# A two-layer diffusion backbone in fp32: the modulation's background steps on another timetable, half of the norm roots on VectorE

## The chip, the cores and the metric

The kernel runs on one core of one Trainium2 chip, as one launch. The metric is the device time of that launch in microseconds. Engines are called as the profile does: PE is TensorE, DVE is VectorE, ACT is ScalarE, POOL is GpSimd, SP is SyncE.

## The reference

Two layers of a backbone for flow matching work on 256 context tokens followed by 512 latent tokens, width 1024, feed-forward width 2816. Each layer has a SwiGLU feed-forward half step, a token mixer, and a second feed-forward half step. Layer 0 mixes with windowed attention beside a chunked spatial gating (gMLP), layer 1 with a bidirectional recurrence. Each of these three parts begins with an RMS norm and is modulated by three vectors (shift, scale, gate) that come from the conditioning vector through a large weight matrix `ada_w` of 1024 x 9216 per layer:

```python
def rmsnorm(x, g):
    xf = x.astype(jnp.float32)
    y = xf * lax.rsqrt(jnp.mean(xf * xf, axis=-1, keepdims=True) + EPS)
    return (y * g.astype(jnp.float32)).astype(x.dtype)

def modulate(h, shift, scale):
    return h * (1.0 + scale) + shift

def ffn_half_step(x, g, shift, scale, gate, wg, wu, wd):
    h = modulate(rmsnorm(x, g), shift, scale)
    return x + 0.5 * gate * swiglu(h, wg, wu, wd)
```

Context tokens use a learned conditioning vector `c_ctx`, so there are two versions of each modulation vector.

## The kernel before, in words

**Products.** All matrices are fp32. `mm3` (L124 ff) makes one product out of three matmuls of high and low halves (`hhi`, `hlo` of the activations, two halves of each weight tile `w`). Most are 128 x 384: the 768 tokens are worked on in two halves, `TA` (tokens 0 to 383) and `TB` (384 to 767). Weights are streamed: SP loads a `raw` chunk (L188), ACT and DVE split it into halves (L198 and L201, or seven combinations in `Seven`, L228 to L245), in a pool of twelve slots. `stream["limit"]` says how many of them may be in use.

**Order.** The program is written out by a Python planner. `mm` adds an estimated time to a clock `clk.t`; after each `mm3`, `clk.tick()` runs the jobs that are due on a heap. Steps of weight preparation, parts of a norm, and the background steps described next are such jobs, so what is written when follows this estimated time. The framework then arranges each engine's instructions once more (one whose inputs are there early can come to stand ahead of others that were written before it); the rows quoted below show that final order, in which each engine runs them.

**Modulation in the background.** `ada_jobs` (L465 ff) computes the modulation vectors (l, m), m from 0 to 8, one after the other in the order of `ada_halves`: layer 0 as 2, 4, 3, 5, 7, 6, 8 (0 and 1 are made at the start), then layer 1. Each needs eight tiles `aw` of 512 KB, loaded by SP into two buffers (`ada_load`), and 32 steps on DVE that multiply a tile by one conditioning value and add it into `acc` (L494, L496, 128 x 512), then transposes and sums (L505, L506) into `red`. `finish` closes a vector: one small matmul of `red` with `quarters` into `ps`, and four additions (L479). `ada_event` (L521 ff) runs one step and puts itself back on the heap: each 1600 ns of planned time until (0,2) is done, then each `bg["every"]`. Whoever needs a vector calls `mod(l, m)` (L527 ff), which runs all the steps that are still missing at that place:

```python
    def mod(l, m):
        while mods_done.get((l, m), 0) < 4:
            ada_step()
        return mods[l][:, m]
```

**Feed-forward.** `ffn(l, j, ...)` (L652 ff) works through groups of the 22 column blocks: products `pgu` for gate and up, `g` on DVE (L682), `ghi`/`glo` (L135, L136), then `down` with products `pd`, whose result is multiplied by the gate vector `gate`. That vector is made at the first `down` by `gates(l, m, .5)` (L643), which calls `mod`; ffn (0,0) needs (0,2), ffn (0,1) needs (0,8). Sums of scaled activations called `form` (L708 to L731) are made on DVE for the products that use seven combinations. In the last group `bg["on"]` is set False, and the next norm is fed.

**Norm.** `Norm` (L545 ff) sums squares, then `stats` (L574 ff) makes the inverse root with `rsqrt` (L142 ff): three operations on DVE and three rounds of Newton's method, each round four operations on POOL (L150, L155, L156, L157), or three on DVE (L150, L152, L153) where the caller asks for it. `spread` takes the root `rstd` to all partitions through TensorE, `apply` and `halve` make the halves. The last `halve` of the second half sets `bg["on"] = not bg["hold"]`.

**Attention and gMLP.** `even_mixer` (L896 ff) has 24 attention units; each ends with a multiplication of the result by the weights of the softmax (L1132, tile `q`), called a gather here. Between them stand the gMLP's row blocks with a root `rs_z` of their own on DVE. In the main program (L1486) the background is switched on with `hold=True`, which stops it when norm (0,1) is through; it stays off through most of the attention.

## Time and profile before

| | |
|---|---|
| median of 3 runs | 2626.02 us (2624.25 to 2627.23) |
| profiled execution | 2622.59 us |
| its span | 2620.8 us |
| mean granted TensorE clock | 0.985 |
| PE busy | 2529.3 us (97%), 14370 matmuls |
| DVE busy | 1869.7 us (71%) |
| ACT busy | 1249.0 us (48%) |
| POOL busy | 238.8 us (9%) |
| DMA | 328.45 MB, 125 GB/s |

The page divides one execution by engine, by line and by wait. A row of a timeline gives the start of an instruction (or of a run of equal ones, with the number behind x), its duration, the engine, the line, output and inputs, and in brackets the idle time ahead of it with the engine and tile that ended it. A granted clock of 1.00 is 2.4 GHz, .50 is 1.2 GHz.

### The profile page before, as it was taken

Reading aid. Unit: us, or ns where it says so; the run is one execution under the profiler, and the core shown is the slowest. Engines: PE = TensorE matmul, PEld = TensorE weight load, DVE = VectorE, ACT = ScalarE, POOL = GpSimd, SP = SyncE. Lnnn points to the kernel's source line nnn. Section 1 sums busy time; section 2 is a strip of 40 time slices with the busy share of each in tenths; the row PEclk is TensorE's granted clock in tenths of the full one; section 3 lists DMA queues with packets and bytes.
Section 4 is the critical chain, followed back from the end, with each engine's and each line's share of the span. In section 5 each row is a group of like instructions: output and inputs, shape, how many; then the busy total and the mean of one; then the engine's idle time right before and its main releaser. Section 6 shows DMA issues by size and latency. Waiting matters only on the chain.

```text
span 2620.8 us, 37768 instructions
## 1 busy us (share of the span) xinstructions
PE 2529.3 (97%) x14370; PEld 2352.3 (90%) x14370; DVE 1869.7 (71%) x3590; ACT 1249.0 (48%) x2433; POOL 238.8 (9%) x389
## 2 busy tenths in 40 slices
PE   8799999999999997999999999999999999999998
PEld 5799999998899996999999889999999988888887
DVE  7778878787668687867768888765467898544444
ACT  3344544545556353444454444444545996433322
POOL 0021012200000002012120020121300000000000
PEclk9999999999999998999999999999999999999999
DMA  9266467653011417556675165673642123322221
GB/s 324 89 144 164 138 157 177 169 172 113 1 33 42 151 51 166 159 142 145 157 165 187 39 176 169 171 191 92 134 145 81 49 75 102 107 97 97 94 89 57
DMA packets 248430, 328.45 MB, mean 125 GB/s; under 512 B 19985, under 2 KB 172729, under 8 KB 247737
## 3 DMA queue, kind: packets, MB, share of 16 engines
q1 hardware_dynamic: 213264, 278.69, 32.8%
q0 software_dynamic: 34560, 47.20, 12.3%
q8 instruction: 112, 1.84, 0.3%
q14 instruction: 70, 0.57, 0.1%
q10 hardware_dynamic: 424, 0.15, 0.0%
HBM read 262.04 MB, written 63.96 MB: 124 GB/s over the span
## 4 chain that ended last, share of the span: by engine, by line
PE 73%; issue 12%; DVE 7%; ACT 4%; POOL 3%; DMA 1%; ACTq 0%; POOLq 0%; DVEq 0%
PE pgu L121 22%; PE pd L121 20%; PE seeded L121 13%; PE ps L121 10%; PE po L121 4%; POOL kept L696 2%; PE pv L121 1%; PE sl L121 1%; PE sc L121 1%; DVE acc L496 1%; PE pt L1111 1%; ACT w L198 1%; DVE w L201 1%; PE pre L121 1%; DVE hlo L607 0%
## 5 line engine op out<-in xcount | busy, mean ns | idle before, releaser
L121 PE MATMUL pd<-ghi,w 128*128 128x256 f32 (+2 forms) x2528 | 649.6, 344 | 2.3 <-ACT ghi L135 2.2
L121 PE MATMUL pgu<-hhi,w 128*128 128x384 f32 (+2 forms) x2144 | 594.5, 349 | 0.9 <-ACT hhi L601 0.6
L121 PEld LDWEIGHTS pd<-ghi,w 128*128 128x128 f32 x2528 | 443.3, 190 | 53.7 <-ACT ghi L135 4.2
L121 PE MATMUL pd<-glo,w 128*128 128x256 f32 (+2 forms) x1264 | 433.6, 344 | 0.8 <-DVE glo L136 0.8
L121 PEld LDWEIGHTS pgu<-hhi,w 128*128 128x128 f32 x2144 | 392.0, 189 | 27.8 <-ACT hhi L601 1.3
L121 PE MATMUL pgu<-hlo,w 128*128 128x384 f32 (+2 forms) x1072 | 374.1, 349 | 1.3 <-DVE hlo L607 1.2
L201 DVE TENSOR_TENSOR w<-raw,w 128x512 fp32r<-128x512 f32 x404 | 271.5, 686 | 92.6 <-ACT w L198 90.1
L198 ACT ACTIVATE w<-raw 128x512 fp32r<-128x512 f32 x404 | 245.7, 626 | 180.4 <-PE pd L121 79.1
L696 POOL DMA_DIRECT2D kept<-add x240 | 208.2, 900 | 1158.7 <-ACT add L695 1150.4
L496 DVE SCALAR_TENSOR_TENSOR acc<-aw,cs,acc 128x512 f32<-128x512 f32 x392 | 280.4, 744 | 33.0 <-DMA aw<-in_ada_w_dram 32.1
L228 DVE TENSOR_TENSOR w<-raw,w 128x512 fp32r<-128x512 f32 x348 | 232.1, 685 | 91.9 <-ACT w L245 88.8
L695 ACT ACTIVATE add<-pd,gate 128x256 f32<-128x256 f32 x240 | 138.7, 580 | 278.0 <-PE pd L121 234.5
L121 PEld LDWEIGHTS pd<-glo,w 128*128 128x128 f32 x1264 | 239.9, 190 | 27.4 <-DVE glo L136 3.2
L121 PE MATMUL seeded<-form,w 128*128 128x384 f32 x1392 | 261.6, 335 | 2.6 <-ACT seeded L790 2.5
L121 PE MATMUL seeded<-hhi,w 128*128 128x384 f32 x928 | 247.8, 335 | 1.4 <-ACT hhi L135 1.0
L121 PEld LDWEIGHTS seeded<-form,w 128*128 128x128 f32 x1392 | 243.1, 188 | 3.5 <-ACT seeded L790 2.8
L245 ACT ACTIVATE w<-raw 128x512 fp32r<-128x512 f32 x348 | 207.1, 627 | 58.4 <-DVE raw L244 17.6
L121 PEld LDWEIGHTS pgu<-hlo,w 128*128 128x128 f32 x1072 | 202.4, 189 | 15.3 <-DVE hlo L607 2.1
L121 PE MATMUL ps<-hhi,w 128*128 128x384 f32 (+1 forms) x704 | 197.6, 355 | 7.6 <-ACT t L1327 6.2
L121 PEld LDWEIGHTS seeded<-hhi,w 128*128 128x128 f32 x928 | 168.6, 188 | 3.4 <-ACT hhi L135 2.5
L121 PE MATMUL seeded<-hlo,w 128*128 128x384 f32 x464 | 155.3, 335 | 0.4 <-DVE hlo L136 0.4
L121 PEld LDWEIGHTS ps<-hhi,w 128*128 128x128 f32 x704 | 132.1, 193 | 15.4 <-ACT t L1327 7.2
(302 smaller groups left out, 3645.0 us busy)
## 6 DMA issues: line engine op xcount, KB each, us to landing
aw<-in_ada_w_dram SPq DMA_DIRECT2D x128, 512.0 KB, 5.2
raw<-in_ffn_w_gate_dram SPq DMA_DIRECT2D x44, 1024.0 KB, 5.6
raw<-in_ffn_w_up_dram SPq DMA_DIRECT2D x44, 1024.0 KB, 5.3
raw<-in_ffn_w_down_dram SPq DMA_DIRECT2D x40, 1024.0 KB, 5.2
kept<-add POOLq DMA_DIRECT2D x120, 256.0 KB, 5.4
kept<-add POOLq DMA_DIRECT2D x120, 128.0 KB, 5.6
x<-kept SPq DMA_DIRECT2D x48, 192.0 KB, 4.2
fw<-in_ada_w_dram SPq DMA_DIRECT2D x16, 512.0 KB, 8.8
```

The source lines that it names most:

```text
L121: pe.matmul(o, w, x, start=start, stop=stop, skip_group_check=again)
L198: act.activation(tiles[i][:, 0:512], self.raw[:, i * 512:i * 512 + 512], AF.Copy)
L201: dve.tensor_tensor(t[:, 512:1024], self.raw[:, i * 512 - 512:i * 512], t[:, 0:512].bitcast(F32), op=ALU.subtract)
L228: dve.tensor_tensor(l, src[key], h.bitcast(F32), op=ALU.subtract)
L245: act.activation(halves_of(key)[0], src[key], AF.Copy)
L496: dve.scalar_tensor_tensor(acc[:, v, :], w[:, k, :], s, acc[:, v, :], op0=ALU.mult, op1=ALU.add)
L695: act.activation(t, ps[:, 0:c1 - c0], AF.Copy, scale=state["gate"][:, 4 * c + d, v:v + 1])
L696: pool.dma_start(out=saved(l, j)[:, 4 * c + d, c0:c1], in_=t, accum_op=ALU.add)
L1111: pe.transpose(ps[:, o:o + 128], self.src[hh][b + bb], ident)
```

## The change

Six places are edited. Background steps come each 900 ns until (0,2) is done, and each 1700 ns afterwards. In the attention they run on each 4800 ns, without `hold`. The root of the second half of each `Norm` runs on DVE. At the end of each feed-forward stage that keeps its norm input (`saving`), not of one stage alone, the limit of weight slots is eight until the next norm is through.

```diff
--- before.py
+++ after.py
@@ -512,7 +512,7 @@
         late.pop(0)()
 
     ada = ada_jobs()
-    bg = {"on": True, "hold": False, "over": False, "every": 2000.0, "sums": False}
+    bg = {"on": True, "hold": False, "over": False, "every": 1700.0, "sums": False}
 
     def ada_step():
         if next(ada, "over") == "over":
@@ -522,7 +522,7 @@
         if bg["on"] and not (bg["sums"] and mods_done.get((0, 2), 0) == 4):
             ada_step()
         if not bg["over"]:
-            clk.at(1600.0 if mods_done.get((0, 2), 0) < 4 else bg["every"], ada_event)
+            clk.at(900.0 if mods_done.get((0, 2), 0) < 4 else bg["every"], ada_event)
 
     def mod(l, m):
         while mods_done.get((l, m), 0) < 4:
@@ -578,7 +578,7 @@
             for i in range(nt):
                 mm(ps[:, i:i + 1], self.ssq[:, i * 128:(i + 1) * 128], ones[:, 0:1], True, True, 4)
             self.r = const.tile([128, 4], F32, tag="rstd" + self.which, name="rstd")
-            rsqrt(ps[:, 0:nt], self.r[:, 0:nt], nt, 1.0 / D, self.which)
+            rsqrt(ps[:, 0:nt], self.r[:, 0:nt], nt, 1.0 / D, self.which, dve if self.c1 == NT else pool)
 
         def prep_mod(self):
             m = mod(self.l, 3 * self.j + 1)
@@ -609,7 +609,7 @@
             self.left -= 1
             if not self.left and self.c1 == NT:
                 bg["on"] = not bg["hold"]
-                if (self.l, self.j) == (1, 0):
+                if stream["limit"] == 8:
                     stream["limit"] = SLOTS
                     pump()
 
@@ -865,7 +865,7 @@
                             down(f0, ng, G, dn[c], c, d, c0, c1)
                             nrm.add(4 * c + d)
                         if end:
-                            if (l, j, c) == (0, 1, 1):
+                            if c == 1 and saving:
                                 stream["limit"] = 8
                             done(dn[c])
                     nrm.run()
@@ -1483,7 +1483,7 @@
 
     halves = (TA, TB)
     norms = ffn(0, 0, halves, [], norm_of(0, 1), {"ahead": 1}, pre)
-    bg.update(on=True, hold=True, every=6000.0)
+    bg.update(on=True, every=4800.0)
     even_mixer(norms)
     norms = project_out(cwo0, halves, gates(0, 5, 1.0), norm_of(0, 2))
     bg.update(hold=False, every=2500.0)
```

Three places of the program show how the instructions move. The first is PE at the end of the last gate/up group of ffn (0,0), where modulation (0,2) is closed (`ps<-red,quarters`) and the down products `pd` begin. Before:

```order
L121 MATMUL pgu<-hhi_163,w 128x384
L121 MATMUL pgu<-hlo_171,w 128x384
L121 MATMUL pgu<-hhi_163,w 128x384
L121 MATMUL seeded<-hhi_156 128x384 x2
L121 MATMUL ps<-red,quarters 128x64
L121 MATMUL pd<-ghi,w 128x256
```

Now:

```order
L121 MATMUL pgu<-hhi_157,w 128x384
L121 MATMUL pgu<-hhi_158,w 128x384
L121 MATMUL pgu<-hlo_166,w 128x384
L121 MATMUL ps<-red,quarters 128x64
L121 MATMUL pgu<-hhi_158,w 128x384
L121 MATMUL pgu<-hhi_159,w 128x384
L121 MATMUL pgu<-hlo_167,w 128x384
```

The closing matmul stands 40 matmuls earlier, between two products of the last `pgu` group; before, it was the last thing ahead of `pd`.

The second is DVE at the first `down` of ffn (0,1), from the last `glo` of the group on to the gate vector `gate` that the down products need. Before:

```order
L136 TENSOR_TENSOR glo<-silu,ghi 128x384
L506 TENSOR_REDUCE red<-acc_t 128x2x8
L494 TENSOR_SCALAR acc<-aw,cs 128x512 x2
L496 SCALAR_TENSOR_TENSOR acc<-aw,cs,acc 128x512 x6
L201 TENSOR_TENSOR w<-raw,w 128x512 x2
L496 SCALAR_TENSOR_TENSOR acc<-aw,cs,acc 128x512 x8
L505 STREAM_TRANSPOSE acc_t<-acc 128x512 x2
L506 TENSOR_REDUCE red<-acc_t 128x2x8 x2
L494 TENSOR_SCALAR acc<-aw,cs 128x512 x2
L496 SCALAR_TENSOR_TENSOR acc<-aw,cs,acc 128x512 x2
L479 TENSOR_TENSOR mods_153<-ps,veca 32x16 x4
L496 SCALAR_TENSOR_TENSOR acc<-aw,cs,acc 128x512
L643 TENSOR_SCALAR gate<-mods_153 128x16
```

Now:

```order
L815 TENSOR_TENSOR uv<-uv 128x384
L201 TENSOR_TENSOR w<-raw,w 128x512 x2
L136 TENSOR_TENSOR glo<-uv,ghi 128x384
L815 TENSOR_TENSOR silu<-seeded,silu 128x384
L201 TENSOR_TENSOR w<-raw,w 128x512 x2
L136 TENSOR_TENSOR glo<-silu,ghi 128x384
L228 TENSOR_TENSOR w<-raw,w 128x512
L237 TENSOR_TENSOR s_10104<-raw 128x512
L239 TENSOR_TENSOR raw<-raw 128x4x128
L228 TENSOR_TENSOR w<-s_10104,w 128x512
L242 TENSOR_TENSOR raw<-raw 128x4x128
```

Behind the last `glo` of the group (`glo<-silu`) stands weight preparation. The run of `acc`, `acc_t` and `red` steps is gone, `gate` itself stands 42 rows ahead of this `glo`, and (0,8) is closed in the attention, some 800 PE rows earlier.

The third is DVE between the root `rs_z` of a gMLP row block and a gather (L1132) near the end of the attention, at the fourth gather from the end before:

```order
L201 TENSOR_TENSOR w<-raw,w 128x512
L148 TENSOR_SCALAR zst<-rs_z 128x1
L150 TENSOR_TENSOR rs_z<-zst 128x1
L152 SCALAR_TENSOR_TENSOR rs_z<-rs_z 128x1
L153 SCALAR_TENSOR_TENSOR zst<-rs_z,zst 128x1
L150 TENSOR_TENSOR rs_z<-zst 128x1
L152 SCALAR_TENSOR_TENSOR rs_z<-rs_z 128x1
L153 SCALAR_TENSOR_TENSOR zst<-rs_z,zst 128x1
L1026 SCALAR_TENSOR_TENSOR gz<-ps,gm,bsB 128x128
L150 TENSOR_TENSOR rs_z<-zst 128x1
L1132 TENSOR_TENSOR q_5712<-pv,w 64x2x128
```

and at the same gather now:

```order
L148 TENSOR_SCALAR zst<-rs_z 128x1
L479 TENSOR_TENSOR mods_153<-ps,veca 32x16
L150 TENSOR_TENSOR rs_z<-zst 128x1
L479 TENSOR_TENSOR mods_153<-ps,veca 32x16
L152 SCALAR_TENSOR_TENSOR rs_z<-rs_z 128x1
L496 SCALAR_TENSOR_TENSOR acc<-aw,cs,acc 128x512
L153 SCALAR_TENSOR_TENSOR zst<-rs_z,zst 128x1
L496 SCALAR_TENSOR_TENSOR acc<-aw,cs,acc 128x512
L150 TENSOR_TENSOR rs_z<-zst 128x1
L496 SCALAR_TENSOR_TENSOR acc<-aw,cs,acc 128x512
L152 SCALAR_TENSOR_TENSOR rs_z<-rs_z 128x1
L1132 TENSOR_TENSOR q_5712<-pv,w 64x2x128
```

Three `acc` steps and the additions that close (0,8) (L479) now stand between the operations of the root. Of the 24 units, those from the sixth to the eleventh and from the eighteenth to the twenty-second have such steps added, one to seven each.

## Rows read from the trace of the kernel before

**Rows 1.** Page, part 1: busy us (share of the span) and instructions by engine.
```profile
PE 2529.3 (97%) x14370; PEld 2352.3 (90%) x14370; DVE 1869.7 (71%) x3590; ACT 1249.0 (48%) x2433; POOL 238.8 (9%) x389
```

**Rows 2.** TensorE's timeline around its two longest stops: start, us, what, count, idle before.
```profile
116.86 0.51 PE L121 MATMUL seeded<-hhi 128*128 128x384 f32 x2
132.19 0.66 PE L121 MATMUL ps<-red,quarters 128*128 128x64 f32 x2 [14.82 <-DVE red L506]
...
983.75 0.33 PE L121 MATMUL seeded<-hlo,w 128*128 128x384 f32 x1
983.92 0.34 PE L121 MATMUL seeded<-hhi,w 128*128 128x384 f32 x1
1001.09 0.69 PE L121 MATMUL ps<-red,quarters 128*128 128x64 f32 x2 [16.83 <-DVE red L506]
```

**Rows 3.** VectorE's timeline, 92 to 136 us, at the first stop.
```profile
92.17 0.56 DVE L682 TENSOR_TENSOR g<-pgu,silu 128x384 f32<-128x384 f32 x1 [6.46 <-PE pgu L121]
...
100.49 0.56 DVE L682 TENSOR_TENSOR g<-pgu,silu 128x384 f32<-128x384 f32 x1 [6.61 <-PE pgu L121]
...
120.83 0.54 DVE L136 TENSOR_TENSOR glo<-g,ghi 128x384 fp32r<-128x384 f32 x1
...
121.77 4.05 DVE L496 SCALAR_TENSOR_TENSOR acc<-aw,cs,acc 128x512 f32<-128x512 f32 x6
...
135.51 0.17 DVE L643 TENSOR_SCALAR gate<-mods 128x16 f32<-128x16 f32 x1
```

**Rows 4.** VectorE's timeline, 986 to 1005 us, at the second stop.
```profile
986.04 0.52 DVE L136 TENSOR_TENSOR glo<-silu,ghi 128x384 fp32r<-128x384 f32 x1
...
987.07 0.87 DVE L494 TENSOR_SCALAR acc<-aw,cs 128x512 f32<-128x512 f32 x2
...
993.28 5.39 DVE L496 SCALAR_TENSOR_TENSOR acc<-aw,cs,acc 128x512 f32<-128x512 f32 x8 [0.15 <-DVE w L201]
...
1003.08 0.71 DVE L479 TENSOR_TENSOR mods<-ps,veca 32x16 f32<-32x16 f32 x4
...
1004.49 0.17 DVE L643 TENSOR_SCALAR gate<-mods 128x16 f32<-128x16 f32 x1
```

**Rows 5.** Windows after both stops: us; engines' busy us; PEclk; DMA share; GB/s.
```profile
130.00:135.00 5.00, 2.81 (x13) 2.84 (x14) 4.93 (x13) 0.00 (x0) 0.00 (x0) 0.50 0.36 108
135.00:140.00 5.00, 5.00 (x20) 4.12 (x20) 5.00 (x9) 0.76 (x2) 1.01 (x1) 0.68 0.65 198
...
1000.00:1005.00 5.00, 3.91 (x16) 3.81 (x17) 4.93 (x13) 0.23 (x1) 0.00 (x0) 0.50 0.44 123
```

**Rows 6.** Groups of L1132, the gathers: ns min/median/max, first and last start.
```profile
L1132 DVE TENSOR_TENSOR q<-pv,w x24: 394/421/428, 643.8 to 847.3; 64x256 f32<-64x256 f32 x24
```

**Rows 7.** Windows of 25 us in the attention, columns as in rows 5.
```profile
700.00:725.00 25.00, 25.00 (x167) 22.82 (x166) 14.57 (x40) 15.21 (x48) 0.00 (x0) 1.00 0.01 2
...
800.00:825.00 25.00, 25.00 (x202) 23.65 (x201) 19.52 (x71) 12.87 (x39) 0.00 (x0) 1.00 0.01 2
825.00:850.00 25.00, 24.07 (x187) 22.90 (x186) 24.03 (x71) 16.36 (x44) 0.00 (x0) 1.00 0.33 86
```

**Rows 8.** SyncE's timeline, 715 to 850 us.
```profile
723.60 0.37 SPq L188 DMA_DIRECT2D raw<-in_ev_w_in_dram  x1
```

**Rows 9.** GpSimd's timeline, second-half root of norm (0,2), first and last of twelve.
```profile
920.69 0.56 POOL L150 TENSOR_TENSOR rs<-rstd 128x3 f32<-128x3 f32 x1 [24.94 <-DVE rstd L148]
...
924.40 0.20 POOL L157 TENSOR_TENSOR rstd<-rstd,rs 128x3 f32<-128x3 f32 x1
```

**Rows 10.** VectorE's timeline, root of the gMLP norm, two of its nine operations.
```profile
775.70 0.16 DVE L150 TENSOR_TENSOR rs_z<-zst 128x1 f32<-128x1 f32 x1
775.89 0.16 DVE L152 SCALAR_TENSOR_TENSOR rs_z<-rs_z 128x1 f32<-128x1 f32 x1
```

**Rows 11.** TensorE's waits on GpSimd: us in total, times, longest.
```profile
PE ps L121 <- POOL rstd L157: 13.1, 9, 2.5
```

**Rows 12.** Page, part 6: modulation weights, count, KB each, median us to landing.
```profile
aw<-in_ada_w_dram SPq DMA_DIRECT2D x128, 512.0 KB, 5.2
```

## The prediction

> **What bounds the kernel now.** I read the page first, then TensorE's waits, then the two largest of them in the timelines and in short windows. The page says that TensorE is the bound: it is busy for 2529.3 of 2620.8 us [rows 1]. A change that leaves its matmuls alone can win only from the 91.5 us left, and from stretches at the lower clock. No matmul is added or removed here, only placed elsewhere.
>
> Of the idle time, two waits hold 31.65 us. TensorE stops at 117.37 and goes on at 132.19, after 14.82 us, and stops at 984.26 until 1001.09, after 16.83 us. Both times it ends the stop with the small matmul on `red` and `quarters` that closes a modulation [rows 2]. The timeline of VectorE shows why: `mod` forces steps. From 121.77 VectorE works off modulation steps, the gate of the down projection follows at 135.51, and the second stop reads the same, from 987.07 to the gate at 1004.49 [rows 3, 4]. The `gate` needs modulation (0,2) in the first case and (0,8) in the second, and both were behind.
>
> Each stop costs more than its idle time, since the clock is down afterwards. From 130 to 135 TensorE has 2.81 us busy at a granted clock of .50 (1.2 instead of 2.4 GHz), from 135 to 140 5.00 us at .68: 2.81 x .50 + 5.00 x .32 = 3.0 us lost. After the second stop it is 3.91 us at .50, 2.0 us [rows 5]. So the first stop is worth 17.8 us and the second 18.8, together 36.6.
>
> **The change part by part.** *Steps at 900 ns until (0,2) is done.* The interval is looked at after each product of three matmuls, so 1600 came out as four products and 900 as two, about 2.08 and 1.04 us of planned time. In the order of the changed program nothing is left to force at the first `down`: the quarters matmul stands 40 matmuls ahead of the end of the gate/up group. 40 matmuls at the .17 us by which such matmuls are spaced (983.75 to 983.92 [rows 2]) put it at about 110.6 us; VectorE, with 17 steps more before that point at .67 each (eight take 5.39 [rows 4]), is ready for it between 109.5 and 111.3 by my count through its new order. It has room: before, it stood idle 6.46 and 6.61 us in front of two `g` [rows 3], and 17 x .67 = 11.4 us go into those 13.1. What remains is what is late next. The last `glo` begins at 120.83 and takes .54 [rows 3], so it is there at 121.4, four microseconds after TensorE's stop at 117.4; the down group can run perhaps 1.4 us without it. That leaves 2.6 us, and 0.9 for VectorE running later than before: 3.5. Gain **14**. Bounds: 17.8 if VectorE is early, 8 if the extra steps push the last `glo` by another 6 us (half of the 11.4).
>
> *Steps through the attention (every 4800, no hold).* Counted between the 24 gathers of attention units (L1132), about 44 `acc` operations, with the closing of (0,8), now run there and shortly behind; the 29 forced steps around 987 go. Again the next late thing is the last `glo`: it begins at 986.04 [rows 4], so TensorE, out of products at 984.3, would wait for it about a microsecond anyway, and in the new order four `acc` and four weight operations more stand ahead of it, 8 x .67 = 5.4 us, of which I take 3.8 as late. Residual 4.8, gain **14**; bounds 18 (nothing late) and 8 (all 5.4 late, the glo's own wait, and a drop of the clock on top).
>
> What the moved steps cost where they now stand: VectorE's gaps. Gathers run from 643.8 to 847.3 [rows 6], 8.8 us apart. From 700 to 725 VectorE is busy 14.57 of 25 us [rows 7], 3.7 us idle per unit; the five steps of such a unit take 3.4, so they cost nothing. In units 12 to 17 nothing is added: the next `aw` tile waits in SyncE's queue behind the loads of the mixer's own weights, of which one of `in_ev_w_in` only goes out at 723.60 [rows 8]; I leave those units alone. Units 19 to 22 get 18 steps and four small additions, 18 x .67 + .7 = 12.8 us. Idle there: 5.48 of 25 from 800 to 825, .97 from 825 to 850 [rows 7], and about 1.1 before 800, 7.5 in all. The overrun of 5.3 lands on TensorE where it waits for softmax operands; some is absorbed in buffers: **-4**, bounds 0 and -12.8 (no gap usable).
>
> *Roots of the second half on VectorE.* On GpSimd the twelve operations take from 920.69 to 924.60, 3.9 us, one of them .56 instead of .20 [rows 9]. On VectorE nine dependent small operations are .19 apart, 9 x .19 = 1.75 [rows 10], if nothing stands between. In the new order the second-half root of norm (0,2) has a 512-wide operation in each of its eight gaps: 8 x .67 = 5.4 with the chain hidden behind them, 7.1 with it added; I take 6.3, so 2.4 us worse. That of norm (0,1) has four small additions (four take .71 [rows 4]) and two `acc` between: 2.1 to 3.8, taken as 3.0, so .9 better. The other three are nearly contiguous, but TensorE's waits on the roots are 13.1 us over nine [rows 11], 1.5 each, and one of the three isn't among them: 2 at most. Sum +.5, taken as **0**, bounds -4 and +3.
>
> *Limit of eight weight slots at other stage ends.* VectorE's weight operations stand at the same places at the ends of ffn (0,0) and (1,0) in both programs: **0**. *Interval 1700 instead of 2000*: both round up to four products: **0**. Queue order: `aw` loads go out earlier on SyncE, at the same number; each is 512 KB with a median of 5.2 us to landing [rows 12] and the 12 steps that now run back to back at 80 to 90 us need three of them with two buffers. I hold at most 3 us of waiting on VectorE there, inside its 13.1 us of idle. Behind the second stop fourteen stand nearly back to back in the new order, for modulation (1,1); what waits there is weight preparation, and I put it inside the bounds.
>
> Sum: 14 + 14 - 4 + 0 = 24. The profiled execution took 2622.6, so 2598.6. It lies 3.4 under the median of the runs, 2626.0, hence **2602.0**.
>
> **The rivals.** *The wait changes its name.* Both stops shrink only by half, since VectorE is the next to be late and TensorE waits for the last `glo` or a form, with the clock falling again. For it: VectorE is busy 24.03 of 25 us in the tail of the attention [rows 7] and has little room around 984. Gain (17.8 + 18.8)/2 - 4 = 14.3: 2611.7. Chance .20.
>
> *Both stops go whole and the attention is free.* Gain 36.6: 2589.4. For it: 10 us of idle VectorE per 25 in half of the attention; against: the last `glo` of both groups [rows 3, 4]. Chance .12.
>
> *The attention pays for everything.* All 44 steps end on TensorE's path, 44 x .67 = 29.5, and TensorE, starved in short stops, runs at .50 for some 20 us, another 10: 2626 - 28 + 39.5 = 2637.5, slower. This decides from the point where VectorE's work per unit exceeds the 8.8 us between gathers in all units; rows show that only in the last three [rows 7]. Chance .03. The Trainium skill (Perfetto Trace Analysis, Optimizing Scalar/DVE Operations) says that work should leave VectorE for ScalarE or GpSimd where VectorE is saturated; this change does the opposite, with steps and with roots. By that rule the 825 to 850 stretch and the second-half root of norm (0,2) should get worse, and the trace agrees for that stretch (24.03 of 25), not for the rest (14.57 of 25 from 700).
>
> *It doesn't do what it says.* The interval of 1700 and the slot limit do nothing, as counted above; should also the moved steps only trade places with products that VectorE makes late, the sum is within 5 us of nothing: 2621 to 2631. Chance .05.
>
> **How the numbers follow.** Forecast .60, half gain .20, full gain .12, nothing .05, attention pays .03. A difference of 0.2%, 5.3 us, is about what can be told from no change, so faster is under 2620.8: .60 + .20 + .12 = .92; same .05; slower .03. The forecast's bounds are 8 + 8 - 9 - 3, which is 4, and 17.8 + 18 + 3; all ends at once are unlikely, and the two stops are independent, so I take 10 to 38 of gain: the range is **2588 to 2616**, which holds the half and the full case and leaves out the last two and the far ends.
>
> **What would show it.** Right: no wait of TensorE on L506 over 5 us, stops at about 117 and 984 of 3 to 6 us on `glo`, a form or the gate; the quarters matmul of (0,8) before 850; VectorE idle under 1 us from 800 to 850 and the span of the attention 2 to 6 us longer; no second-half root on GpSimd. Wrong: a stop at 117 of more than 8 us (steps late for lack of `aw`), the clock at .50 anywhere from 780 to 850, or idle gaps on `acc` waiting for its DMA in the middle of a root's chain.

## The result, and the profile after

The changed kernel takes 2605.06 us (median of 4, 2604.11 to 2606.45) against 2625.14 us before (median of 4, 2623.76 to 2627.23). The ratio is 0.9923, 95% interval 0.9906 to 0.994: 20 us faster. Forecast were 2602 us and a range of 2588 to 2616. The profiled execution took 2604.11 us, its span is 2602.3 us, 18.5 under that of before.

Both long stops are gone. TensorE's timeline of the changed kernel shows the closing matmul of (0,2) after a wait of 0.71 us, and the down products directly behind the last `pgu`; the first down product of ffn (0,1) starts at 978.72 with no idle time ahead of it. These rows answer to [rows 2]:

```profile
110.09 0.43 PE L121 MATMUL ps<-red,quarters 128*128 128x64 f32 x2 [0.71 <-DVE red L506]
...
117.20 0.33 PE L121 MATMUL pgu<-hhi,w 128*128 128x384 f32 x1
117.38 0.28 PE L121 MATMUL pd<-ghi,w 128*128 128x256 f32 x1
...
978.72 0.28 PE L121 MATMUL pd<-ghi,w 128*128 128x256 f32 x1
```

The clock is at 1.00 where it was .50 to .68 in [rows 5] (windows; us, busy us of PE, PEld, DVE, ACT, POOL, PEclk, DMA share, GB/s):

```profile
115.00:120.00 5.00, 5.00 (x33) 4.77 (x32) 4.95 (x13) 1.60 (x4) 0.00 (x0) 1.00 0.05 14
120.00:125.00 5.00, 4.99 (x28) 4.16 (x27) 4.97 (x12) 2.86 (x6) 0.03 (x1) 1.00 0.00 0
```

TensorE's waits, whole run (engine, tile and line waited for, us in total, times, longest). L506 is down to 0.7 us, from the two waits of 14.82 and 16.83 us of [rows 2]; GpSimd's roots cost 9.0 in five waits, where [rows 11] has 13.1 in nine; a wait of 2.8 us on a root on VectorE is new:

```profile
PE ps L121 <- POOL rstd L157: 9.0, 5, 2.5
...
PE ps L121 <- DVE ssq L572: 4.5, 3, 1.5
...
PE ps L121 <- DVE rstd L153: 2.8, 1, 2.8
...
PE ps L121 <- DVE red L506: 0.7, 1, 0.7
```

Where the 18.5 us come from shows in the start of the same matmul in both traces. "Ahead" is before minus after, so a number that rises from one row to the next is a gain between the two:

| matmul (n-th row of its kind) | before, us | after, us | ahead |
|---|---|---|---|
| first `pgu<-hlo` | 62.80 | 62.08 | 0.7 |
| 25th `pd<-ghi`, behind the first stop | 140.87 | 123.29 | 17.6 |
| 13th `sl`, start of the attention | 679.18 | 663.38 | 15.8 |
| first `po`, end of the attention | 846.22 | 833.32 | 12.9 |
| 301st `pgu<-hlo`, behind norm (0,2) | 950.58 | 944.24 | 6.3 |
| 318th `pgu<-hlo`, ahead of the second stop | 976.47 | 971.10 | 5.4 |
| 720th `pd<-ghi`, behind the second stop | 1007.25 | 982.37 | 24.9 |
| 1291st `pd<-ghi`, end of ffn (0,1) | 1423.07 | 1403.20 | 19.9 |
| last `pd<-ghi` | 2609.20 | 2590.73 | 18.5 |

So the two stops gave 16.9 and 19.5 us, the attention took 2.9, the stretch around norm (0,2) 6.6, and what follows the second stop 6.4. The rest is small: 0.7 won ahead of the first row, 1.8 lost between the first stop and the attention, 0.9 ahead of the second stop. This table is called the ledger below; one execution stands in each column.

The page of the changed kernel, part 1, against [rows 1], tells the same in two numbers:

```profile
PE 2534.7 (97%) x14370; PEld 2356.5 (91%) x14370; DVE 1875.2 (72%) x3635; ACT 1246.4 (48%) x2433; POOL 227.5 (9%) x329
```

TensorE idles 23.9 us less (91.5 before, 67.6 now), but the same matmuls keep it busy 5.4 us longer. The low clock behind the two stops is gone, but low clock elsewhere, as at norm (0,2) below, has taken its place.

### The profile page after: what moved, and what is told of

Read it like the earlier page. It is cut to its first block, busy times and chain, and to the rows that moved or that the text cites. A ratio compares the mean times of both kernels' runs of the same rounds, so it can differ in the third digit from the quotient of the medians.

```text
span 2602.3 us, 37742 instructions
## 1 busy us (share of the span) xinstructions
PE 2534.7 (97%) x14370; PEld 2356.5 (91%) x14370; DVE 1875.2 (72%) x3635; ACT 1246.4 (48%) x2433; POOL 227.5 (9%) x329
## 5 line engine op out<-in xcount | busy, mean ns | idle before, releaser
L121 PE MATMUL pd<-glo,w 128*128 128x512 f32 (+2 forms) x1264 | 431.4, 342 | 0.6 <-DVE glo L136 0.6
L228 DVE TENSOR_TENSOR w<-raw,w 128x512 fp32r<-128x512 f32 x348 | 232.2, 687 | 108.2 <-ACT w L245 105.9
```

The lines of the kernel that those rows point to most:

```text
L121: pe.matmul(o, w, x, start=start, stop=stop, skip_group_check=again)
L228: dve.tensor_tensor(l, src[key], h.bitcast(F32), op=ALU.subtract)
```

## The experiments

The kernel before was run again beside each set of runs, and its median differs from the 2625.1 us that the expectations start from (2622.7 in the first set); so gains are compared below, each within its set, and not times. The first four take the change apart. `only_900`, `only_4800` and `only_roots` are the kernel before with one edit; `no_roots` is the changed kernel without one.

```diff
only_900:   +            clk.at(900.0 if mods_done.get((0, 2), 0) < 4 else bg["every"], ada_event)
only_4800:  +    bg.update(on=True, every=4800.0)
only_roots: +            rsqrt(..., self.which, dve if self.c1 == NT else pool)
no_roots:   -            rsqrt(..., self.which, dve if self.c1 == NT else pool)
            +            rsqrt(..., self.which)
```

> The kernel before, with the 900 ns interval alone. Theory (each stop goes with its own edit): the stop at 117 us and the low clock behind it go whole, 17.6 us, the stop of 16.8 us at the first down of ffn (0,1) stays; 2625.1 - 17.6 = 2607.5 (2604.5 to 2610.5). Rival (the early pace also shortens the later forced run, since one stream of steps feeds both): the second stop shrinks by several us too, 2603 or less. Second rival (the first stop only moves to the last glo): 2612 or more.

Measured: 2608.06 against 2622.71, ratio 0.9945 (0.9927 to 0.9964), a gain of 14.6 us where 17.6 were expected, at the low end of the range. By the ledger the first stop gives 15.8 (2.1 ahead at the first `pgu`, 17.9 behind the stop), and the second stop stays at 16.9 us of waiting on L506. The theory holds, a little smaller than forecast; the two stops don't share their steps.

> The kernel before, with the background running through the attention each 4800 ns without hold, alone. Theory (the steps between attention and second stop cost where VectorE's short root operations wait behind them): the second stop goes (-18.9), the attention pays 3.4, the first-half root of norm (0,2) and later stages 4 to 8; 2625.1 - 18.9 + 3.4 + 6 = 2615.6 (2612 to 2619). Rival (what is lost between 846 and 974 us belongs to the roots on VectorE, not to the steps): 2625.1 - 15.5 = 2609.6 or less. The first stop of 14.8 us stays in both.

Measured: 2618.98, ratio 0.9985 (0.9972 to 0.9998), a gain of 3.7 us. The expectation had 9.5 (6 to 13) and missed, in the direction of its own theory: the losses around the steps are larger than it took them. The rival had 15.5 and is out. The ledger of the profiled execution (2622.47 us, one of its longer ones): 4.5 lost in the attention (1.3 behind at its start, 5.8 at its end), 4.3 around norm (0,2), 2.5 on to 976 us, 19.5 won at the stop, then 6.8 lost on the way to the last matmul. With every root still on GpSimd the second-half root of norm (0,2) got worse than before; TensorE waits 3.8 us for it here, 3.5 in `no_roots` below, where the same steps stand beside it, and 2.3 before. GpSimd's timeline there in `only_4800`:

```profile
929.09 0.56 POOL L150 TENSOR_TENSOR rs<-rstd 128x3 f32<-128x3 f32 x1 [27.52 <-DVE rstd L148]
929.73 0.58 POOL L155 TENSOR_TENSOR rs<-rs 128x3 f32<-128x3 f32 x1
930.40 1.18 POOL L156 TENSOR_SCALAR rs<-rs 128x3 f32<-128x3 f32 x1
931.66 0.19 POOL L157 TENSOR_TENSOR rstd<-rstd,rs 128x3 f32<-128x3 f32 x1
...
933.87 0.20 POOL L157 TENSOR_TENSOR rstd<-rstd,rs 128x3 f32<-128x3 f32 x1
```

And the windows of the root and behind it in the same kernel, columns as above:

```profile
930.00:935.00 5.00, 1.16 (x6) 0.89 (x5) 1.52 (x3) 0.79 (x2) 3.24 (x11) 0.83 0.39 105
935.00:940.00 5.00, 5.00 (x18) 5.00 (x18) 4.20 (x9) 2.06 (x4) 0.00 (x0) 0.50 0.00 0
```

Three of the first operations take .56, .58 and 1.18 us where the same take .19 or .20 in the last rounds, with no operation of VectorE beside them; the chain takes 4.98 instead of 3.9 us, TensorE waits 3.8 us and then runs at .50. Beside the three stand 512-wide operations on VectorE, two of weight preparation and two background steps (the .56 is in [rows 9] too, beside weight preparation alone). The Trainium skill (SBUF — State Buffer, SBUF: two separate sides) says that VectorE and GpSimd share a port pair that an operation of either locks for its whole length while the other blocks, on VectorE's side for instance an operation with two SBUF inputs; the lengthened operations agree with that.

> The kernel before, with the second half's roots on VectorE alone. Theory (a root on VectorE is quick where no background step stands between its operations): no steps run at norm (0,2) here, so that root ends 1 to 2 us sooner, that of norm (0,1) 2.3; 2620 to 2623. Rival (VectorE is a worse place for a root of norm (0,2) whatever the steps do): that root ends later by 2 us with a lower clock behind it, 2626 to 2629.

Measured: 2618.17, ratio 0.9981 (0.997 to 0.9992), a gain of 4.5 us where 2 to 5 were expected; the rival is out. No step stands at norm (0,2) in this order, and from the end of the attention to the 301st `pgu<-hlo` the kernel wins 1.6 us (2.3 behind the kernel before, then 0.7); across norm (0,1), from the 664th `pd<-ghi` ahead of it to the first `sl`, it wins 0.7.

> The changed kernel with all roots back on GpSimd. Theory: 2.3 us lost at norm (0,1), 3 us won at the second-half root of norm (0,2) (3.9 instead of 5.9 us, no drop of the clock), about 1 lost at the others: 2605 plus or minus 2. Rival (the roots edit is what costs between 846 and 974 us): 2599 or less. Second rival (roots on VectorE are worth what TensorE waited for them on GpSimd): 2609 or more.

Measured: 2610.53, ratio 0.9951 (0.9935 to 0.9967), a gain of 12.2 us where 20 were expected. The expectation missed; the time is the second rival's (the roots are worth what TensorE waited for on GpSimd). Its profile, though, lost about 5 us before any root (12.9 ahead at the 25th `pd<-ghi`, where the changed kernel has 17.6): part of the first stop was back with 3.9 us, since VectorE waited 3.4 us for an `aw` tile at 60 to 116 us. That wait differs between executions of the same order: 1.9 in the changed kernel, 4.0 in a later run (`pause_e40`), and TensorE's wait goes with it. VectorE's and TensorE's waits in `pause_e40`, 60 to 116 and 100 to 125 us:

```profile
DVE acc L496 <- DMA aw<-in_ada_w_dram: 4.0, 1, 4.0
...
PE ps L121 <- DVE red L506: 4.3, 1, 4.3
```

So `no_roots` shows that the roots gain, not how much: across norm (0,1) it loses 2.1 us (10.2 to 8.1 ahead) where the changed kernel wins 0.3, and its other losses aren't all the roots'. Around norm (0,2) the edit shows no price in either direction: from the end of the attention to the 301st `pgu<-hlo` `no_roots` takes 110.3 us, the changed kernel 110.9 in one execution and 108.2 in another (`again`, below).

Across norm (0,1), between the two matmuls named above, all fourteen profiles can be compared: 95.7 to 100.1 us in the five with both roots on GpSimd, 94.0 to 95.6 in the eight with the second on VectorE, 89.7 in the one with both there (`pause_all`, below). The kernel before has the shortest of the five, so its profile alone understates what this root gains.

What was left open by these four is why norm (0,2) loses 6.6 us in the changed kernel. VectorE's timeline of the changed kernel there shows nine root operations, from 911.77 to 917.61, 5.84 us, with a 512-wide operation in each of the eight gaps, five background steps and three of weight preparation:

```profile
911.77 0.15 DVE L150 TENSOR_TENSOR rs<-rstd 128x3 f32<-128x3 f32 x1
911.84 0.75 DVE L496 SCALAR_TENSOR_TENSOR acc<-aw,cs,acc 128x512 f32<-128x512 f32 x1
912.50 0.15 DVE L152 SCALAR_TENSOR_TENSOR rs<-rs 128x3 f32<-128x3 f32 x1
912.58 0.74 DVE L496 SCALAR_TENSOR_TENSOR acc<-aw,cs,acc 128x512 f32<-128x512 f32 x1
...
917.46 0.15 DVE L153 SCALAR_TENSOR_TENSOR rstd<-rs,rstd 128x3 f32<-128x3 f32 x1
```

The windows behind the two roots of that norm, in the changed kernel, show the clock down, at the first half (root on GpSimd in both kernels) as at the second:

```profile
885.00:890.00 5.00, 5.00 (x23) 5.00 (x23) 3.15 (x9) 2.91 (x7) 0.00 (x0) 0.66 0.02 3
...
915.00:920.00 5.00, 2.33 (x9) 2.33 (x10) 4.58 (x12) 0.00 (x0) 0.00 (x0) 0.68 0.36 105
920.00:925.00 5.00, 5.00 (x21) 5.00 (x20) 5.00 (x10) 3.22 (x6) 0.00 (x0) 0.64 0.32 105
```

At .66, .68 and .64 with 5.00, 2.33 and 5.00 us busy, 5.00 x .34 + 2.33 x .5 + 5.00 x .36 is 4.7 us lost (.50 taken for the middle one, whose first half is idle time at full clock). The next runs take the background steps away from there, and test the edits that were forecast at nothing.

```diff
again:     the changed kernel
pause:     +    bg["on"] = False
                norms = project_out(cwo0, halves, gates(0, 5, 1.0), norm_of(0, 2))
no_limit:  -                if stream["limit"] == 8:
           +                if (self.l, self.j) == (1, 0):
           -                            if c == 1 and saving:
           +                            if (l, j, c) == (0, 1, 1):
no_1700:   -    bg = {..., "every": 1700.0, ...}
           +    bg = {..., "every": 2000.0, ...}
```

> The changed kernel once more, as the yardstick for the three beside it: 20 us under the kernel before, as measured (2625.1 to 2605.1); both theories agree. If the stop at 117 us depends on when the weight tiles land, its profile shows a wait of up to 4 us on L506 there.

Measured: 2604.34 against 2623.2, ratio 0.992 (0.9907 to 0.9932). The wait on L506 at 117 us is 2.0 us in its profile. This second execution of the same program also says how far the losses at norm (0,2) repeat: TensorE waits as long on both roots there (2.54 and 2.81 us; 2.55 and 2.81 in the first), but behind the first the clock doesn't fall, and behind the second it falls for a shorter time. The stretch that lost 6.6 us loses 3.8. The same windows in `again`:

```profile
885.00:890.00 5.00, 4.60 (x28) 4.60 (x29) 3.59 (x10) 2.95 (x7) 0.26 (x2) 1.00 0.09 30
...
915.00:920.00 5.00, 3.11 (x14) 3.11 (x15) 5.00 (x12) 1.28 (x3) 0.00 (x0) 0.77 0.42 121
920.00:925.00 5.00, 5.00 (x28) 5.00 (x27) 5.00 (x11) 2.51 (x6) 0.00 (x0) 0.88 0.23 88
```

> The changed kernel with the background switched off from the end of the attention to the end of norm (0,2). Theory (background steps among the short operations of the roots of norm (0,2) make both late and drop the clock): both roots end sooner, no clock of .64 to .68 at 885 to 925 us, 5 to 6 us faster than the changed kernel. Rival (VectorE's root is long whatever stands beside it): the same time, within 2 us. Second rival (the steps left out come back as a wait at the next gate, (1,2)): slower by 2 us or more at the end of ffn (1,0).

Measured: 2590.66, ratio 0.9869 (0.9854 to 0.9884): 13.7 us faster than the changed kernel in the same comparison, more than twice what was expected. TensorE waits 1.5 us on the first root of norm (0,2) and not at all on the second, and the clock stays up. VectorE's timeline of `pause` at the second-half root:

```profile
909.46 0.15 DVE L150 TENSOR_TENSOR rs<-rstd 128x3 f32<-128x3 f32 x1
909.53 0.17 DVE L643 TENSOR_SCALAR gate<-mods 128x16 f32<-128x16 f32 x1
909.65 0.16 DVE L152 SCALAR_TENSOR_TENSOR rs<-rs 128x3 f32<-128x3 f32 x1
...
911.75 0.15 DVE L153 SCALAR_TENSOR_TENSOR rstd<-rs,rstd 128x3 f32<-128x3 f32 x1
```

The windows at both roots of norm (0,2) in `pause`:

```profile
885.00:890.00 5.00, 5.00 (x31) 5.00 (x30) 4.07 (x12) 3.29 (x8) 0.00 (x0) 1.00 0.12 42
...
910.00:915.00 5.00, 5.00 (x31) 4.74 (x30) 4.63 (x14) 2.83 (x7) 0.00 (x0) 1.00 0.00 2
```

By the ledger the stretch from the end of the attention to the 301st `pgu<-hlo` now wins 1.7 us (12.2 to 13.9 ahead) where the changed kernel loses 6.6, or 3.8 in `again`. The rest of the gain lies behind the second stop, where the kernel with the pause loses 1.5 us to the end and the changed kernel 6.4 (2.5 in the profile of `again`); the steps there fall on other instructions, and no single wait holds it. That part isn't settled. The steps left out came back as no wait: L506 has 1.8 us in the whole run.

> The changed kernel with the two edits of the slot limit undone. Theory (the edit does nothing, VectorE's weight operations stand at the same places): within 2 us of the changed kernel, and the span from 846 to 974 us the same to 1 us. Rival (fewer weights ahead of norm (0,2) and in ffn (0,1) are what the changed kernel loses behind 846 us): 4 us or more faster.

Measured: 2601.96, ratio 0.9919 (0.9905 to 0.9933). The same as `again` within the intervals (2.4 us by the medians), and from the end of the attention to the second stop both profiles take 135.0 us. The rival is out.

> The changed kernel with 2000 ns again in place of 1700. Theory: nothing in ffn (0,0) rests on it, within 2 us of the changed kernel. Rival (the modulations come later by a few steps, so that (0,8) closes later and its steps fall into the full tail of the attention): 3 us or more slower, with more VectorE work from 800 to 850 us.

Measured: 2603.42, ratio 0.9932 (0.9919 to 0.9945). The same, within the intervals. In the order, though, 1700 does move something: the closing matmuls of layer 0 stand up to 43 matmuls earlier with it, and at the second-half root of norm (0,2) TensorE waits 5.1 us without it and 2.8 with it, for a chain of 5.84 us in both (more on this under `pause_all`). It is a small edit without a measurable price, not one without effect.

The last four ask whether number or place of the steps costs, and what the roots are worth once no step stands between their operations. All but `dense` contain the pause.

```diff
dense:      +    bg["every"] = 2400.0
                 norms = project_out(cwo0, halves, gates(0, 5, 1.0), norm_of(0, 2))
pause_pool: -            rsqrt(..., self.which, dve if self.c1 == NT else pool)
            +            rsqrt(..., self.which)
pause_all:  +            rsqrt(..., self.which, dve)
pause_e40:  -    bg.update(on=True, every=4800.0)
            +    bg.update(on=True, every=4000.0)
```

> The changed kernel with the background at 2400 instead of 4800 during the output projection: 20 modulation operations run between the attention and the second gate instead of 16, but in the final order none of them stands between the operations of either root of norm (0,2). Theory (it is the place among a root's short operations that costs, not the number of steps): both roots as quick as with the pause, 5 us or more faster than the changed kernel, ratio to the kernel before .990 or less. Rival (steps cost by their number, on a VectorE that is full from 850 to 975 us): slower than the changed kernel, ratio .993 or more.

Measured: 2591.03 against 2624.54, ratio 0.9867 (0.985 to 0.9883). More steps than in the changed kernel, and as fast as the pause. It is the place that costs. The profiles agree: from the end of the attention to the 301st `pgu<-hlo` the four with the second-half root on VectorE and no step among its operations (`pause`, `dense`, `only_roots`, `pause_e40`) take 102.7 us each, the four with steps there (the changed kernel, `again`, `no_limit`, `no_1700`) 108.2 to 110.9. Which place a step gets is set by the order, which the interval only shifts; 2400 moves the steps past the root that 4800 puts them into.

> The kernel with the pause, with all roots back on GpSimd. Theory (with no step among its operations a root on VectorE ends 2 us sooner): 4 to 7 us slower than with the pause (ratio to the kernel before .989 to .990). Rival (the pause alone is what helps, the engine of the root doesn't matter): within 2 us of the pause.

Measured: 2598.02, ratio 0.9895 (0.9879 to 0.991), 7 us behind `pause` by the medians, at the edge of what the two intervals (of two comparisons) tell apart. It agrees with 13.1 us of waits on GpSimd's roots in its profile against 7.9 with the pause.

> The kernel with the pause, with the roots of both halves on VectorE. Theory: TensorE still waits 7.9 us in five waits on GpSimd's roots of the first halves; each chain gets 1.5 to 2 us shorter where VectorE has no other work between, 4 us faster than the pause (ratio about .985). Rival (other VectorE work gets between, as at the second half of norm (0,2) in the changed kernel): same or slower than the pause.

Measured: 2577.0 (2575.87 to 2578.28), ratio 0.9816 (0.9801 to 0.9832). This is the fastest version, 47.5 us under the kernel before, and by the medians of the two comparisons it won 13.7 us over the pause where 4 were expected. The page of `pause_all`, part 1:

```profile
PE 2523.0 (98%) x14370; PEld 2347.0 (91%) x14370; DVE 1880.3 (73%) x3680; ACT 1245.2 (48%) x2433; POOL 209.9 (8%) x269
```

The window at the first-half root of norm (0,1) in `pause_all`:

```profile
565.00:570.00 5.00, 4.78 (x30) 4.48 (x29) 4.34 (x12) 0.53 (x1) 0.00 (x0) 1.00 0.07 17
```

The two windows at the same root in the changed kernel:

```profile
562.00:567.00 5.00, 2.47 (x13) 2.15 (x12) 2.22 (x4) 0.87 (x2) 2.92 (x10) 0.82 0.34 105
567.00:572.00 5.00, 5.00 (x26) 5.00 (x26) 3.25 (x9) 3.56 (x8) 0.00 (x0) 0.84 0.00 0
```

The changed kernel waits 2.5 us for GpSimd there and goes on at a lower clock; with the root on VectorE TensorE idles .22 us in the window and the clock stays. Against `pause`, whose span is 15.5 us longer, TensorE idles 9.6 us less by the two pages (61.1 to 51.5; 7.5 of it are waits on roots) and is busy 5.9 us less with the same matmuls. By the ledger `pause_all` is 1.6 us ahead of `pause` in front of norm (0,1), for reasons that aren't the roots'; it gains 4.3 across norm (0,1), 1.8 more up to behind norm (0,2), 3.2 net from there to the output projection of layer 1, and 3.7 at norm (1,2).

The theory (a shorter chain) explains only part of this. At the first half of norm (0,2) the chain is shorter: TensorE has the same 21 products between the last sum of squares and the matmul that takes the root (`ps<-ident,rstd`, the spread), the root is there 3.0 us behind the sums instead of 5.4, and the wait of 1.5 us is gone. At the first half of norm (0,1), where most is won, it isn't. VectorE's timeline of `pause_all` there has a long operation in every gap, as at norm (0,2) of the changed kernel, and the root takes 5.84 us from its first operation to its last, longer than on GpSimd (4.5):

```profile
562.72 0.15 DVE L150 TENSOR_TENSOR rs<-rstd 128x3 f32<-128x3 f32 x1
562.79 0.75 DVE L496 SCALAR_TENSOR_TENSOR acc<-aw,cs,acc 128x512 f32<-128x512 f32 x1
563.45 0.15 DVE L152 SCALAR_TENSOR_TENSOR rs<-rs 128x3 f32<-128x3 f32 x1
563.52 0.55 DVE L572 TENSOR_TENSOR ssq<-ssq,sq 128x384 f32<-128x384 f32 x1
...
568.41 0.15 DVE L153 SCALAR_TENSOR_TENSOR rstd<-rs,rstd 128x3 f32<-128x3 f32 x1
```

What changed there is TensorE's own order: more products stand between the sums and the spread. TensorE's timelines at the spread, in `pause` and in `pause_all`:

```profile
568.38 0.96 PE L121 MATMUL ps<-ident,rstd 128*128 128x128 f32 x6 [2.52 <-POOL rstd L157]
...
568.71 0.91 PE L121 MATMUL ps<-ident,rstd 128*128 128x128 f32 x6 [0.22 <-DVE rstd L153]
```

| root | last sum to root, us | matmuls between | TensorE's wait, us |
|---|---|---|---|
| norm (0,1), first half, `pause` (GpSimd) | 6.5 | 21 | 2.5 |
| the same, `pause_all` (VectorE) | 8.4 | 45 | 0.2 |
| norm (0,2), second half, changed kernel | 8.2 | 29 | 2.8 |
| the same, `no_1700` | 8.2 | 16 | 5.1 |
| the same, `pause` | 4.8 | 26 | none |

Roots that are about equally late cost 0.2, 2.8 or 5.1 us, by how many products, of some .18 us each, the order puts ahead of the spread. Why the order does so was not tested, and no run changes the engine of a root and leaves TensorE's order alone; how the 13.7 us divide between the shorter chains and the other order is open.

> The kernel with the pause and an interval of 4000 in the attention instead of 4800: the last five units then hold no modulation operations, (0,8) closes before them. Theory (the 3 us that the attention lost are lost in the units 19 to 22, where VectorE has no idle time): 2 to 3 us faster than the pause. Rival (the loss lies in the steps themselves, wherever they stand in the attention): same as the pause within 1 us; or, if eight steps in one unit overrun it, slower.

Measured: 2591.93, ratio 0.9867 (0.9846 to 0.9888), as with the pause. In its profile the attention costs 0.7 us (11.1 ahead at its start, 10.4 at its end) instead of 2.4 with the pause, which is the way the theory has it, but the `aw` wait of 4.0 us above fell on this execution, and the times can't tell 2 us. Unsettled.

## Why the prediction was right, point by point

The total was forecast at 24 us and came out at 20, inside the range. That it came this near is in part luck: the gains at the stops were 8.4 us larger than forecast, and losses of some 13 us at norm (0,2) and behind the second stop, for which the sum had 0, cancelled them. The signs that were to show it right came (no wait on L506 over 5 us, (0,8) closed at 806 us, VectorE idle 0.3 and 0.7 us in the last two windows of the attention, no second-half root on GpSimd), except for the stops of 3 to 6 us on the last `glo`; and one sign of being wrong came too, a clock of .50 in the attention (below).

**The two stops, 14 each.** That the forced steps were what held TensorE, that the edits of 900 and 4800 take them away one by one, and that the low clock goes with them was right (`only_900`, `only_4800`). The size failed at "What remains is what is late next", with 3.5 and 4.8 us left for the last `glo`. Nothing is left: 16.9 and 19.5 us were won, where the prediction priced the whole stops at 17.8 and 18.8. The quarters matmul of (0,2) came at 110.09, as counted. VectorE did make the last `glo` late, as counted, in both places:

```profile
122.96 0.55 DVE L136 TENSOR_TENSOR glo<-g,ghi 128x384 fp32r<-128x384 f32 x1
...
123.90 0.16 DVE L643 TENSOR_SCALAR gate<-mods 128x16 f32<-128x16 f32 x1
...
981.66 0.56 DVE L136 TENSOR_TENSOR glo<-silu,ghi 128x384 fp32r<-128x384 f32 x1
```

In the first place it is ready at 123.5, six microseconds after TensorE began the down products at 117.38 (the `gate` follows at 123.90, and TensorE doesn't need it, only the operations that read its results out do). But the order of the down products puts those of column blocks and token halves that are ready ahead of the rest, so TensorE ran on: 5.00 and 4.99 us busy in the two windows from 115 to 125 above. "The down group can run perhaps 1.4 us without it" was the wrong sentence; it ran about six, and at the second stop 3.5 (from 978.72 to 982.2).

**The attention, -4.** 2.9 us in the ledger, with VectorE at 24.66 and 24.31 of 25 us and the clock at .93 in the last window, so the overrun of the last units is real ([rows 7] had .97 and 5.48 us idle in two such windows). At .50 from 825 to 828 us TensorE, busy throughout, loses 1.5 us; `pause`, with the same order in the attention, has no such fall and still loses 2.4. The windows of the changed kernel:

```profile
790.00:815.00 25.00, 24.32 (x194) 22.83 (x193) 24.66 (x81) 13.26 (x39) 0.00 (x0) 1.00 0.15 43
815.00:840.00 25.00, 23.95 (x165) 22.68 (x164) 24.31 (x69) 17.40 (x43) 0.00 (x0) 0.93 0.51 138
825.00:828.00 3.00, 3.00 (x16) 3.00 (x16) 3.00 (x14) 2.88 (x9) 0.00 (x0) 0.50 0.35 106
```

**The roots, 0.** At norm (0,1) the second-half chain takes 3.46 us (forecast 3.0) where GpSimd took 3.9. TensorE's wait there falls by more than that, from 1.75 us to .05, since 29 matmuls instead of 22 stand between the sums and the spread in the new order, which the prediction didn't look at. For the second half of norm (0,2) the mechanism was right: 5.84 us for the chain, forecast 6.3. The price went by the chain alone (+2.4), and two things were left out of it. TensorE's order again has more products ahead of the spread (29 instead of 19), so the wait grew by .6 only, from 2.25 to 2.81 us. And the clock fell behind it, which it had not done before: the last two of the three lines worked out above are 3.0 us, 1.7 in `again`. So the term of -2.4 measured -3.6 in one execution and -2.3 in the other, by another way than forecast. The first-half root, on GpSimd in both kernels, isn't in the sum at all; there `acc` steps between VectorE's preparing operations and beside GpSimd's made a wait of 2.5 us where .8 stood before, and in the first execution another fall of the clock, 1.7 us. Together that is 7.0 us against 6.6 in the ledger, and 4.0 against 3.8 in `again`.

**The limit and 1700, 0.** Right as times (`no_limit`, `no_1700`). "Both round up to four products" holds for the 384-wide products alone, so the order is not the same (see `no_1700`).

**The sum's own arithmetic.** 9 x .19 is 1.71, not 1.75; nine root operations with nothing between take 1.73 us in the changed kernel (1449.50 to 1451.23). The lower end of the bounds takes -9 and -3 for the attention and the roots, whose own terms say -12.8 and -4; with these it is -0.8 instead of 4. The range begins at a gain of 10 and isn't touched by either.

**Left out.** 5 us behind the second stop, between 982 and 1403 us, which the prediction put "inside the bounds". The trace shows there a handful of small waits of TensorE, on sums of the norm (2.9 of the 4.5 us on L572 above) and on operands from VectorE and ScalarE. They change between executions (2.5 instead of 6.4 us to the end in `again`, 9.5 in `no_limit`); that background steps ahead of VectorE's other work make them was argued, and no run isolates it.

The rivals: the wait did not change its name at the stops (half gain), but it did at norm (0,2). Of "both stops go whole and the attention is free" the first half came true; what keeps the kernel from its 2589 us lies at norm (0,2) and behind. "The attention pays" was wrong by more than a factor of ten. The Trainium skill (Perfetto Trace Analysis, Optimizing Scalar/DVE Operations) puts the rule that the prediction names more carefully: where VectorE is saturated, handing work to ScalarE or even GpSimd may make sense, and between VectorE and GpSimd it might not help, as they share a read port. At norm (0,2) the runs agree with the second half: with the steps in place the root costs about as much on GpSimd (`no_roots`) as on VectorE. The best version, with every root on VectorE, says nothing against the rule: VectorE is busy 73% there and not saturated.

## What to carry to other kernels

Work that may run any time should be kept away from the short dependent chains that the bottleneck engine waits for; eight long operations between nine small ones, five of them background steps, make 1.7 us into 5.84. What such a chain costs is set by the order of the engine that waits as well: count the work that stands between the place where the chain starts and the place where its result is taken. A forced catch-up in front of a stage is visible as one long wait on a small matmul, and spreading it out is worth all of it when the products behind can be taken in the order in which their inputs come. Price a wait with the clock behind it, and take that price from more than one execution: from `pause` to `pause_all` TensorE's idle time fell by 9.6 us, and its busy time with the same matmuls by another 5.9.

## What the runs showed of the hardware that was not expected

- Small GpSimd operations on 128x3 tiles take .19 us alone and up to 1.18 us beside VectorE's 512-wide steps and weight operations (`only_4800`).
- A short wait can cost as much again in clock, but doesn't each time: the wait on the root at 882 us in the changed kernel (2.5 us) was followed by a window at .66 in one execution and by one at 1.00 in another (`again`), that of 1.5 us at the same root in `pause` by one at 1.00, and that of 3.8 us at the second-half root in `only_4800` by one at .50. A gain worked out from waits alone can come out too small, and one profile doesn't tell how much.
- Executions with the same order up to that place differ by some us in the time at which one 512 KB `aw` tile is there: VectorE's wait for it at 60 to 116 us was 1.9 to 4.0 us in eleven profiles. With it up to 4.3 us of the first stop come back (0.7 to 2.0 where the wait was 1.9 to 2.1).
